# The state of a two-direction RWKV recurrence kept compact, its products over array quarters

## The chip, the cores and the metric

The kernel runs on one core of one Trainium2 chip, as one program. The metric is the device time of one execution in microseconds (us), the median of three runs. All arithmetic of the part in question is fp32.

## What is computed

The program is a transformer layer (a half feed-forward, a mixer of three attentions, another half feed-forward) followed by a second layer for the same 256 tokens of width 1024: a mixer of a long convolution ("hyena") and an RWKV-7 recurrence, then 16 experts that each choose 32 tokens. The change touches the recurrence alone. It runs twice: once over the 256 context tokens, for their final states only, and once over the 256 tokens of `x`, starting from those states and reading out every token. Each run goes in both directions, for 8 heads with a 64 x 64 state each.

```python
RW_HEADS = 8
RW_HEAD = 64
SCAN_DIRECTIONS = (False, True)

def rwkv_scan(decay, k, v, a_vec, b_vec, r, state0, reverse):
    emit = r is not None
    ...
    def step(S, inp):
        w_t, k_t, v_t, a_t, b_t = inp[:5]
        sa = jnp.einsum('bhij,bhj->bhi', S, a_t)
        S = S * w_t[:, :, None, :] + sa[..., None] * b_t[:, :, None, :] + v_t[..., None] * k_t[:, :, None, :]
        y = jnp.einsum('bhij,bhj->bhi', S, inp[5]) if emit else None
        return S, y
    S, ys = lax.scan(step, state0, xs, reverse=reverse)

def layer(x, ctx, c, c_ctx, p, ctx_out):
    ...
    ctx_states = rwkv_context_states(cols, p, zero_state)
    h = rmsnorm(x, p['norm1_pre']) * (1.0 + m_lat[1]) + m_lat[0]
    mixed, _ = token_mixer_2(h, p, ctx_states)
    x = x + m_lat[2] * rmsnorm(mixed, p['norm1_post'])
    h2 = rmsnorm(x, p['norm2_pre']) * (1.0 + m_lat[4]) + m_lat[3]
    x = x + m_lat[5] * rmsnorm(expert_choice_moe(h2, p), p['norm2_post'])
```

## The kernel before

The recurrence is worked in chunks of 64 tokens (`CH`), four steps (`NCH`) per run. In each step both directions advance by one chunk, the forward one from the front, the backward one from the back, so that the two chunks of a step always lie in opposite halves of the 128 partitions (`r`). Eight heads are kept as four pairs `p` with two heads `e` each; a feature lies on partition `e*64 + i`.

`rwkv` (L942) has three parts. First, for each direction and each half of the tokens, `elementwise` (L1009) forms decays and keys on ACT, DVE and POOL, and `products` (L1064) forms what doesn't depend on the state: masked 64 x 64 products (L1079), the transposed keys `TB` and `kt` (L1090, L1093), the products `MV` (L1098, evacuated at L1103), and the key-value products of both chunks, `pk` (L1109). These are 64 x 128 x 128 (contraction, rows of the output, columns): a pair of heads at a time, of which only the two diagonal 64 x 64 blocks are wanted; four ACT copies of 64x256 take them into `KV` (L1115). Second, a triangular solve: 31 rounds of a DVE product and sum (L1136, L1138), with trips through DRAM before and after (L1129, L1139, L1143), and block products (L1167, L1175) whose evacuations (L1182, L1184) finish the tiles `W`.

Third, the four steps (L1201 on). The state of a direction is a block-diagonal tile of 128 x 4 x 2 x 64, half of it zeros, in a ring of two (`ring`, zeroed at L1193, loaded from `Sctx` at L1191). A step multiplies the state by the decay and adds `KV` on POOL, in halves (`se`, L1213 and L1215, eight instructions of 64x256), multiplies the state by the inputs (`pu`, L1218, eight products of 128 x 64 x 128), adds `MV` on DVE (`u`, L1221), multiplies by `W` (`pz`, L1227, sixteen products of 64 x 64 x 64), copies on ACT (`z`, L1230, a copy for each direction), forms the update (`pn`, L1236, eight products of 64 x 128 x 128, half of each unused), and adds `se` to its diagonal blocks on DVE (L1240, four of 64x256). The run over `x` also adds the state's and `z`'s shares to the output banks `psY` (L1245, L1250). `psT` and `psX` are pools of two PSUM banks each.

The order of work on each engine is made by a list scheduler from the program order and a timing model, with no order written out here; each engine then takes its list in order. The context run (`context_states`, L1261) is issued after the fifth block of the first feed-forward and lies beside that feed-forward's products (L299 to L302 for weight blocks of 256 columns, each weight split on ACT and DVE, L245 and L246) and the first projections of the attention (L287 to L289). The run over `x` (called in `mixer2`, L1471) lies beside the projections and the transform of the long convolution (L1382 to L1434), whose splits are shared by DVE and POOL (L271, L272), and later beside the gate projections. After `psY` comes a normalisation (L1531 on), the output projection, the router, and the experts, whose 384 weight blocks of 1 MB come on SP's queue (L1774) through a ring of SBUF slots.

## Time and profile before

| what | value |
|---|---|
| median of three runs | 2164.89 us (2160.2 to 2174.39) |
| the profiled execution's own time | 2165.86 us |
| its span, first to last instruction | 2164.1 us |
| outside the span | 1.8 us |
| TensorE's mean granted clock, of full speed | 0.868 |
| busy: PE, PEld, DVE, ACT, POOL | 80%, 48%, 41%, 27%, 16% of the span |

PE is TensorE's matmul, PEld its weight load, DVE VectorE, ACT ScalarE, POOL GpSimd, SP SyncE. An fp32 product of the code is two MATMUL records. A row of windows gives the stretch (us from the span's start), its length, then the busy us (and instructions) of PE, PEld, DVE, ACT and POOL, TensorE's granted clock as a share of full speed, the DMA engines' busy share and GB/s. Windows of a line alone give the engines that it uses, then clock and DMA of the whole stretch. A row of a timeline gives start, duration, engine, line, operation, output and inputs, shapes (a product's as contraction*rows, then the moving operand), a count, and in brackets the idle time before it. A row of the chain gives start, duration, engine, tile, line.

### The profile page before, as it was taken

Reading aid. Unit: us, or ns where it says so; the run is one execution under the profiler, and the core shown is the slowest. Engines: PE = TensorE matmul, PEld = TensorE weight load, DVE = VectorE, ACT = ScalarE, POOL = GpSimd, SP = SyncE. Lnnn points to the kernel's source line nnn. Section 1 sums busy time; section 2 is a strip of 40 time slices with the busy share of each in tenths; the row PEclk is TensorE's granted clock in tenths of the full one; section 3 lists DMA queues with packets and bytes.
Section 4 is the critical chain, followed back from the end, with each engine's and each line's share of the span. In section 5 each row is a group of like instructions: output and inputs, shape, how many; then the busy total and the mean of one; then the engine's idle time right before and its main releaser. Section 6 shows DMA issues by size and latency. Waiting matters only on the chain.

```text
span 2164.1 us, 28403 instructions
## 1 busy us (share of the span) xinstructions
PE 1736.5 (80%) x11441; PEld 1048.8 (48%) x11442; DVE 885.5 (41%) x1611; ACT 579.1 (27%) x938; POOL 335.5 (16%) x332
## 2 busy tenths in 40 slices
PE   7999989999988999898898876666666665766675
PEld 5889867777768887887577511111111110111110
DVE  4668765875758665687756400000000000000001
ACT  3346443544436544454323200000000000000000
POOL 2111013210325640235233200000000000000000
PEclk9999998999999999999898887877777768677766
DMA  9665555454448855534445899999999999999996
GB/s 303 217 184 142 159 147 177 138 146 127 136 146 269 274 194 174 156 94 124 121 137 218 338 420 420 420 420 420 420 420 420 419 420 419 420 420 420 420 419 270
DMA packets 187894, 600.95 MB, mean 278 GB/s; under 512 B 35384, under 2 KB 91217, under 8 KB 138610
## 3 DMA queue, kind: packets, MB, share of 16 engines
q1 hardware_dynamic: 151312, 551.89, 67.5%
q0 software_dynamic: 10496, 36.08, 5.0%
q10 hardware_dynamic: 25954, 11.16, 1.9%
q8 instruction: 90, 1.47, 0.3%
q14 instruction: 42, 0.34, 0.0%
HBM read 593.25 MB, written 9.75 MB: 279 GB/s over the span
## 4 chain that ended last, share of the span: by engine, by line
DMA 45%; PE 37%; DVE 9%; ACT 3%; issue 3%; POOL 2%; ACTq 0%; DVEq 0%; SPq 0%; POOLq 0%
DMA ring<-exp_w 42%; PE mm L302 4%; PE mm L301 4%; PE mm L299 4%; PE mm L287 3%; PE mm L288 3%; PE mm L289 3%; DVE wl L246 3%; PE mm L346 2%; PE mm L349 2%; PE mm L345 2%; DMA wraw<-w_in 1%; ACT wh L245 1%; PE mm L254 1%; PE px L839 1%
## 5 line engine op out<-in xcount | busy, mean ns | idle before, releaser
L1789 PE MATMUL px<-ring,xeT 128*32 128x512 f32 x2048 | 356.7, 789 | 185.2 <-DMA ring<-exp_w 185.2
L246 DVE TENSOR_TENSOR wl<-wraw,wh 128x1024 fp32r<-128x1024 f32 (+2 forms) x243 | 317.2, 1307 | 167.4 <-ACT wh L245 163.3
L245 ACT ACTIVATE wh<-wraw 128x1024 fp32r<-128x1024 f32 (+2 forms) x243 | 254.5, 1048 | 372.4 <-PE mm L301 156.0
L302 PE MATMUL mm<-hh,wl 128*128 128x256 f32 x912 | 267.0, 294 | 16.5 <-DVE wl L246 15.5
L1789 PEld LDWEIGHTS px<-ring,xeT 128*32 128x32 f32 x2048 | 49.9, 122 | 465.5 <-DMA ring<-exp_w 390.1
L299 PE MATMUL mm<-hh,wh 128*128 128x256 f32 x912 | 265.4, 292 | 2.7 <-ACT hh L245 2.4
L301 PE MATMUL mm<-hl,wh 128*128 128x256 f32 x912 | 263.5, 289 | 1.9 <-DVE hl L246 1.7
L1825 PE MATMUL tr<-ring,hid 128*32 128x512 f32 x1024 | 182.1, 813 | 101.8 <-DMA ring<-exp_w 89.1
L1801 DVE SCALAR_TENSOR_TENSOR mth<-mth,px 128x512 f32<-128x512 f32 x16 | 11.0, 687 | 556.7 <-ACT mth L1800 556.7
L302 PEld LDWEIGHTS mm<-hh,wl 128*128 128x128 f32 x912 | 178.4, 196 | 31.6 <-DVE wl L246 20.4
L299 PEld LDWEIGHTS mm<-hh,wh 128*128 128x128 f32 x912 | 179.0, 196 | 12.1 <-issue 6.9
L301 PEld LDWEIGHTS mm<-hl,wh 128*128 128x128 f32 x912 | 179.2, 197 | 7.0 <-issue 4.1
L1829 ACT ACTIVATE ye<-tr 128x512 f32<-128x512 f32 x16 | 9.6, 597 | 559.6 <-PE tr L1825 559.6
L1635 POOL TENSOR_SCALAR rsz<-ss 128x1 f32<-128x1 f32 x2 | 0.6, 300 | 930.8 <-ACT ring L1635 930.7
L1825 PEld LDWEIGHTS tr<-ring,hid 128*32 128x32 f32 x1024 | 26.1, 127 | 238.1 <-DMA ring<-exp_w 209.5
L288 PE MATMUL mm<-wl,hh 128*128 128x512 f32 (+2 forms) x320 | 128.2, 401 | 3.5 <-DVE wl L246 2.0
L289 PE MATMUL mm<-wh,hl 128*128 128x512 f32 (+2 forms) x320 | 126.0, 394 | 0.0
L287 PE MATMUL mm<-wh,hh 128*128 128x512 f32 (+2 forms) x320 | 119.3, 405 | 5.2 <-DVE wi L525 3.3
L1802 DVE SCALAR_TENSOR_TENSOR mth<-mth,px 128x512 f32<-128x512 f32 x16 | 11.0, 688 | 252.6 <-PE px L1789 252.6
L1800 ACT ACTIVATE mth<-px 128x512 f32<-128x512 f32 x16 | 9.5, 597 | 281.2 <-PE px L1789 281.2
L288 PEld LDWEIGHTS mm<-wl,hh 128*128 128x128 f32 x320 | 61.4, 192 | 18.9 <-DVE wl L246 3.2
L287 PEld LDWEIGHTS mm<-wh,hh 128*128 128x128 f32 x320 | 59.4, 193 | 20.5 <-issue 7.7
(757 smaller groups left out, 2661.9 us busy)
## 6 DMA issues: line engine op xcount, KB each, us to landing
ring<-exp_w SPq DMA_DIRECT2D x384, 1024.0 KB
wraw<-w_in SPq DMA_DIRECT2D x107, 512.0 KB
mraw<-mod_w POOLq DMA_DIRECT2D x48, 512.0 KB, 5.2
wraw<-ffn_w_gate SPq DMA_DIRECT2D x44, 512.0 KB
wraw<-ffn_w_up SPq DMA_DIRECT2D x44, 512.0 KB
wraw<-ffn_w_down SPq DMA_DIRECT2D x44, 512.0 KB
wraw<-w_out SPq DMA_DIRECT2D x11, 512.0 KB
skew<-bd POOLq DMA_DIRECT2D x1, 3840.0 KB, 26.0
```

The costliest lines, as they stand in the source:

```text
L245: S.activation(dst_h, src, AF.Copy)
L246: (eng or V).tensor_tensor(dst_l, src, dst_h.bitcast(F32), op=ALU.subtract)
L287: PE.matmul(ps[t], hh[:, k, sl], wh, start=(k == 0), stop=False)
L288: PE.matmul(ps[t], hh[:, k, sl], wl, start=False, stop=False)
L289: PE.matmul(ps[t], hl[:, k, sl], wh, start=False, stop=(k == kc - 1))
L299: PE.matmul(o(c), wh[:, cs], hh[:, k, :], start=(k == 0 and bank0(c)), stop=False, skip_group_check=True)
L301: PE.matmul(o(c), wh[:, cs], hl[:, k, :], start=False, stop=False, skip_group_check=True)
L302: PE.matmul(o(c), wl[:, cs], hh[:, k, :], start=False, stop=(k == KC - 1), skip_group_check=True)
L345: PE.matmul(acc[t][nh], fh[:, sl], wh[:, ns], start=(k == 0), stop=False)
L346: PE.matmul(acc[t][nh], fh[:, sl], wl[:, ns], start=False, stop=False)
L1789: PE.matmul(ps[32 * g:32 * g + 32, :], xeT[:, k, es], wt[:, 0, g * 512:(g + 1) * 512], start=(k == 0), stop=(k == KC - 1), skip_group_chec ...
L1825: PE.matmul(pe2[32 * c:32 * c + 32, :], hid[:, 2 * h + j, 32 * g:32 * g + 32], w2t[:, j * 2 + nh, :], start=(g == 0 and h == 0), stop=(g = ...
```

## The change

The state of both directions becomes one compact tile `S_` of 128 x 2 x 4 x 64 without zeros. `pu` becomes sixteen products of 64 x 64 x 64 into two banks, by head of the pair `e` (the row half of the array), with one DVE sum for each bank. The key-value products leave `products`: the transposed keys of both directions stay in `KT`, and each step starts two banks `pn` with sixteen key-value products of 64 x 64 x 64; the update products, sixteen of 64 x 64 x 64, add to the same banks. In both, `p`, `d`, `e` are run through so that four products in a row use the four quarters of the array, each row half with a bank of its own. `se` becomes one POOL product of 128x512, `z` one ACT copy, the new state two DVE sums of 128x256. `MV` is sorted by steps, so that its evacuation is two ACT copies of 64x512 instead of one of 128x512. The last step of the run over `x` forms no new state. The run over `x` keeps block-diagonal copies `Sb` of the state for the `psY` products, made by four ACT copies of 64x256 in each of three steps; at the start, four memsets and five DMAs instead of two and two. The compact tiles take the SBUF of `e` and `kt` (the latter is also the solve's `pr`), the copies that of the old ring.

```diff
-        MV = [(stage or rp).tile([128, 2, 512], F32, name=f"MV{d}") for d in range(2)]
-        KV = [(stage or rp).tile([128, NCH, 4, 64], F32, name=f"KV{d}") for d in range(2)]
+        MV = [(stage or rp).tile([128, 2, 512], F32, name=f"MV{i}") for i in range(NCH // 2)]
+        KT = [(stage or rp).tile([128, 2, 512], F32, name=f"KV{d}") for d in range(2)]
...
-            kt = rp.tile([128, 512], F32, name="kt")
-            V.tensor_copy(kt, f2(ps))
+            V.tensor_copy(KT[d][:, t, :], f2(ps))
...
-            S.activation(MV[d][:, t, :], ps, AF.Copy)
-            pk = [psT.tile([128, 4, 128], F32, name="tr"), psX.tile([128, 4, 128], F32, name="px")]
-            for p in range(4):
-                hs = slice(p * 128, p * 128 + 128)
-                for cc in range(2):
-                    r = slice(cc * 64, cc * 64 + 64)
-                    PE.matmul(pk[cc][:, p, :], kt[r, hs], vt[r, t, hs], start=True, stop=True, skip_group_check=True)
             for cc in range(2):
-                ps = pk[cc]
+                r = slice(cc * CH, cc * CH + CH)
                 step = t * 2 + cc if d == 0 else NCH - 1 - (t * 2 + cc)
-                for e_ in range(2):
-                    f = slice(e_ * 64, e_ * 64 + 64)
-                    S.activation(KV[d][f, step], ps[f, :, e_ * 64:e_ * 64 + 64], AF.Copy)
+                S.activation(MV[step // 2][r, step % 2, :], ps[r], AF.Copy)
...
-        ring = [[rp.tile([128, 4, 2, 64], F32, name="S_", tag=tg) for tg in tgs]
-                for tgs in (("thw0", "tha0"), ("lam0", "km0"))]
-        for i, r_ in enumerate(ring):
-            for d, q_ in enumerate(r_):
-                if i == 1 and S0 is not None:
-                    S.dma_start(q_.rearrange("p a b c -> p (a b c)"), S0[d])
-                else:
-                    G.memset(q_, 0.0)
+        ring = [rp.tile([128, 2, 4, 64], F32, name="S_", tag=tg) for tg in ("e", "kt")]
+        blk = []
+        if emit:
+            blk = [[rp.tile([128, 4, 2, 64], F32, name="Sb", tag=tg) for tg in tgs]
+                   for tgs in (("thw0", "tha0"), ("lam0", "km0"))]
+            for q_ in blk[0] + blk[1]:
+                G.memset(q_, 0.0)
+            S.dma_start(ring[1].rearrange("p a b c -> p (a b c)"), Sctx)
+            for d in range(2):
+                for e in range(2):
+                    f = slice(e * 64, e * 64 + 64)
+                    S.dma_start(blk[1][d][f, :, e, :], Sctx[f, d * 256:d * 256 + 256].rearrange("f (p v) -> f p v", p=4))
...
-        S_ = ring[1] if S0 is not None else None
-
-        def ev(st):
-            return st.rearrange("p e v -> p (e v)")
+        S_ = ring[1] if emit else None
+        def pev(ap):
+            return ap.rearrange("q (p e v) -> q p e v", e=2, v=64)
...
-            u, z = uu[:, step % 2], zz[:, step % 2]
+            u, z, mv = uu[:, step % 2], zz[:, step % 2], MV[step // 2][:, step % 2]
+            ends = emit and step == NCH - 1
+            if not ends:
+                pn = [psX.tile([128, 4, 64], F32, name="px") for _ in range(2)]
+                def to_state(left, right, first):
+                    for p in range(4):
+                        for d, t, r in where:
+                            for e in range(2):
+                                hs = slice((2 * p + e) * 64, (2 * p + e) * 64 + 64)
+                                PE.matmul(pn[d][e * 64:e * 64 + 64, p, :], left(d, t)[r, hs], right(t)[r, hs],
+                                          start=(first and p == 0), stop=not first, skip_group_check=True)
+                to_state(lambda d, t: KT[d][:, t], lambda t: vt[:, t], True)
             if S_ is not None:
-                se = rp.tile([128, 2, 4, 64], F32, name="se", tag="nn")
-                pu = psT.tile([128, 512], F32, name="tr")
-                for d, t, r in where:
+                if not ends:
+                    se = rp.tile([128, 2, 4, 64], F32, name="se", tag="nn")
+                    G.tensor_tensor(se, S_, EC[:, :, :, step:step + 1].to_broadcast([128, 2, 4, 64]), op=ALU.mult)
+                pu = [psT.tile([128, 4, 64], F32, name="tr") for _ in range(2)]
+                for p in range(4):
                     for e in range(2):
                         f = slice(e * 64, e * 64 + 64)
-                        G.tensor_tensor(se[f, d], S_[d][f, :, e, :],
-                                        EC[f, d, :, step:step + 1].to_broadcast([64, 4, 64]), op=ALU.mult)
-                        G.tensor_tensor(se[f, d], se[f, d], KV[d][f, step], op=ALU.add)
-                for p in range(4):
-                    for d, t, r in where:
-                        PE.matmul(pu[r, p * 128:p * 128 + 128], AR[t, d][:, p, 0, r], ev(S_[d][:, p]), start=True,
-                                  stop=True, skip_group_check=True)
-                for d, t, r in where:
-                    V.tensor_tensor(u[r], pu[r], MV[d][r, t, :], op=ALU.add)
+                        for d, t, r in where:
+                            PE.matmul(pu[e][r, p, :], AR[t, d][f, p, 0, r], S_[f, d, p, :], start=True, stop=True,
+                                      skip_group_check=True)
+                for e in range(2):
+                    V.tensor_tensor(pev(u)[:, :, e], pu[e], pev(mv)[:, :, e], op=ALU.add)
+            else:
+                u = mv
             pz = psT.tile([128, 512], F32, name="tr")
             for h in range(8):
                 hs = slice(h * 64, h * 64 + 64)
                 for d, t, r in where:
-                    ur = u[r] if S_ is not None else MV[d][r, t, :]
-                    PE.matmul(pz[r, hs], W[t, d][r, h % 2, h // 2, 0, :], ur[:, hs], start=True, stop=True,
+                    PE.matmul(pz[r, hs], W[t, d][r, h % 2, h // 2, 0, :], u[r, hs], start=True, stop=True,
                               skip_group_check=True)
-            for d, t, r in where:
-                S.activation(z[r], pz[r], AF.Copy)
-            Sn = ring[step % 2]
-            pn = [psX.tile([128, 4, 128], F32, name="px") for _ in range(2)]
-            for p in range(4):
-                hs = slice(p * 128, p * 128 + 128)
-                for d, t, r in where:
-                    PE.matmul(pn[d][:, p, :], TB[d][r, t, hs], z[r, hs], start=True, stop=True, skip_group_check=True)
-            for d, t, r in where:
-                for e in range(2):
-                    f = slice(e * 64, e * 64 + 64)
-                    V.tensor_tensor(Sn[d][f, :, e, :], pn[d][f, :, e * 64:e * 64 + 64],
-                                    se[f, d] if S_ is not None else KV[d][f, step], op=ALU.add)
+            S.activation(z, pz, AF.Copy)
+            if not ends:
+                to_state(lambda d, t: TB[d][:, t], lambda t: z, False)
+                Sn = ring[step % 2]
+                for d in range(2):
+                    if S_ is not None:
+                        V.tensor_tensor(Sn[:, d], pn[d], se[:, d], op=ALU.add)
+                    else:
+                        V.tensor_copy(Sn[:, d], pn[d])
             if emit:
+                Sb = blk[(step + 1) % 2]
                 for p in range(4):
                     for d, t, r in where:
-                        PE.matmul(psY[t][r, p * 128:p * 128 + 128], AR[t, d][:, p, 1, r], ev(S_[d][:, p]),
-                                  start=False, stop=False, skip_group_check=True)
+                        PE.matmul(psY[t][r, p * 128:p * 128 + 128], AR[t, d][:, p, 1, r],
+                                  Sb[d][:, p].rearrange("q e v -> q (e v)"), start=False, stop=False,
+                                  skip_group_check=True)
                 for h in range(8):
                     hs = slice(h * 64, h * 64 + 64)
                     for d, t, r in where:
                         PE.matmul(psY[t][r, hs], W[t, d][r, h % 2, h // 2, 1, :], z[r, hs], start=False,
                                   stop=False, skip_group_check=True)
+                if not ends:
+                    for d in range(2):
+                        for e in range(2):
+                            f = slice(e * 64, e * 64 + 64)
+                            S.activation(blk[step % 2][d][f, :, e, :], Sn[f, d], AF.Copy)
             S_ = Sn
...
-    Sctx = dram.tile([2, 128, 512], F32, name="Sctx")
+    Sctx = dram.tile([128, 512], F32, name="Sctx")
...
-            S_, _, _, _ = rwkv(rp, c, None, zk, zv, zl, None, None)
-            for d in range(2):
-                S.dma_start(Sctx[d], S_[d].rearrange("p a b c -> p (a b c)"))
+            S_, _, _, _ = rwkv(rp, c, None, zk, zv, zl, None)
+            S.dma_start(Sctx, S_.rearrange("p a b c -> p (a b c)"))
```

## Rows read from the trace of the kernel before

**Rows 1.** The page's chain that ended last, by engine

```profile
DMA 45%; PE 37%; DVE 9%; ACT 3%; issue 3%; POOL 2%; ACTq 0%; DVEq 0%; SPq 0%; POOLq 0%
```

**Rows 2.** Windows by stage, all engines: see the columns above

```profile
150.00:217.00 67.00, 66.40 (x785) 61.97 (x785) 52.73 (x73) 43.21 (x93) 11.37 (x15) 1.00 0.47 133
...
307.00:365.00 58.00, 49.75 (x370) 39.32 (x369) 33.61 (x59) 20.31 (x33) 24.00 (x31) 0.88 0.33 93
950.00:1020.00 70.00, 65.15 (x837) 58.81 (x836) 53.04 (x78) 33.22 (x70) 35.85 (x33) 0.96 0.44 120
...
1056.00:1083.00 27.00, 20.34 (x333) 13.89 (x331) 15.91 (x33) 5.17 (x14) 6.74 (x7) 0.81 0.34 89
1083.00:1141.00 58.00, 56.94 (x507) 45.79 (x508) 31.30 (x47) 16.81 (x22) 21.48 (x28) 1.00 0.41 137
...
1244.00:2146.00 902.00, 590.05 (x3181) 102.12 (x3178) 39.25 (x80) 25.57 (x49) 0.00 (x0) 0.75 1.01 418
```

**Rows 3.** Windows of L1109 alone, the key-value products

```profile
150.00:217.00 67.00, 3.97 (x48) 3.20 (x48) 1.00 0.47 133
...
950.00:1020.00 70.00, 5.40 (x64) 4.25 (x64) 0.96 0.44 120
```

**Rows 4.** Windows of L1218 alone, the state products `pu`

```profile
307.00:365.00 58.00, 4.13 (x48) 2.95 (x48) 0.88 0.33 93
...
1083.00:1141.00 58.00, 4.72 (x48) 3.25 (x48) 1.00 0.41 137
```

**Rows 5.** Windows of L1236 alone, the update products `pn`

```profile
307.00:365.00 58.00, 8.79 (x64) 7.63 (x64) 0.88 0.33 93
...
1083.00:1141.00 58.00, 9.24 (x64) 7.71 (x64) 1.00 0.41 137
```

**Rows 6.** Timeline of PE: batches of small products

```profile
163.61 0.97 PE L1079 MATMUL px<-ar,tha 64*64 64x64 f32 x32
...
1077.27 1.29 PE L1175 MATMUL px<-nb,Bs 32*32 32x32 f32 x128
...
1084.83 1.16 PE L1236 MATMUL px<-zk,tb 64*128 64x128 f32 x8
...
1096.86 1.15 PE L1227 MATMUL tr<-uu,nb 64*64 64x64 f32 x32
```

**Rows 7.** Chain of waits, full-size products behind a small batch

```profile
1098.01 0.43 PE mm L287
1098.44 0.23 PE mm L288
```

**Rows 8.** Timeline of POOL, 305 to 330 us

```profile
316.20 0.61 POOL L1213 TENSOR_TENSOR se<-S__2191,ec 64x256 f32<-64x256 f32 x1
...
318.94 0.56 POOL L217 TENSOR_TENSOR rsi<-rsz,power 128x1 f32<-128x1 f32 x1
```

**Rows 9.** Timeline of POOL, 974 to 1008 us

```profile
988.43 1.75 POOL L1213 TENSOR_TENSOR se<-S__10208,ec 64x256 f32<-64x256 f32 x2
990.26 2.23 POOL L1215 TENSOR_TENSOR se<-se,KV 64x256 f32<-64x256 f32 x2
992.57 1.89 POOL L1048 TENSOR_TENSOR x<-x,zk 128x512 f32<-128x512 f32 x1
```

**Rows 10.** Timeline of POOL, 1052 to 1090 us: one 128x512 operation

```profile
1064.43 1.26 POOL L1421 TENSOR_TENSOR yf<-yf,hyt 128x512 f32<-128x512 f32 x1
```

**Rows 11.** Groups by line and shape, 900 to 1180 us: evacuations of `pk`

```profile
L1115 ACT ACTIVATE KV<-px 64x256 f32<-64x256 f32 x8 | 3.0, 379 | 0.1
```

**Rows 12.** Timelines of DVE, then ACT, around the solve's end

```profile
1055.40 0.19 DVE L1138 TENSOR_TENSOR tx<-tx,pr 128x31 f32<-128x31 f32 x1
...
1080.21 1.30 ACT L1182 ACTIVATE nb<-px 32x256 f32<-32x256 f32 x4 [8.82 <-DVE nb L1184]
```

**Rows 13.** Timeline of DVE, the last step's state sums

```profile
1135.13 0.87 DVE L1240 TENSOR_TENSOR S__10208<-px,se 64x256 f32<-64x256 f32 x2
```

**Rows 14.** Timeline of SP: the expert weights' stream

```profile
1150.91 147.92 SPq L1774 DMA_DIRECT2D ring<-exp_w  x54
```

More of the change, by code (lines that the diff above doesn't have):

```diff
@@ L940, in mix_take, with rwkv @@
         return take
-    def rwkv(rp, c, zr, zk, zv, zl, S0, alt, stage=None):
+    def rwkv(rp, c, zr, zk, zv, zl, alt, stage=None):
         emit = zr is not None
@@ L1470, in mixer2 @@
                 rp = f2.enter_context(tc.tile_pool(name="rw", bufs=1))
-                _, psY, vt, prod = rwkv(rp, c, zr, zk, zv, zl, [Sctx[0], Sctx[1]],
+                _, psY, vt, prod = rwkv(rp, c, zr, zk, zv, zl,
                                         [x_[:, h * 512:h * 512 + 512].rearrange("p (a b) -> p a b", a=4)
```

## The prediction, made before the changed kernel was run

> **What bounds the kernel now.** I read the chain that ended last first: waits for DMA hold 45% of the span, TensorE 37%, all else little [rows 1]. Then the windows by stage, to see where each of the two rules. From 1244 us to 2146 us the DMA engines are busy without a gap at 418 GB/s [rows 2]: the experts' weights set the end there, and nothing in the recurrence can shorten that stretch. But the stream's first issue is at 1150.91 us [rows 14], behind the whole mixer, so a stage ahead of it that ends sooner moves the stream, and the end with it, by as much. In the stages ahead TensorE rules, not evenly: it is busy 66.40 of 67 us where the context run forms its products, 49.75 of 58 where its steps run, 65.15 of 70 where the products for `x` are formed, 20.34 of 27 in the solve's tail, and 56.94 of 58 where the steps for `x` run beside the gate projections [rows 2]. Where it is full, a microsecond of products less is a microsecond less; where it waits, what ends the waits has to be looked at.
>
> **The products that go.** The change replaces three kinds. Key-value products, L1109: the 48 records from 150 to 217 us take 3.97 us, 83 ns each, so the context run's 64 take about 5.3 us; for `x` 64 take 5.40 us [rows 3]. State products, L1218: 4.13 us for the context's three steps, 4.72 us for three of the four steps for `x` [rows 4]. Update products, L1236: 8.79 and 9.24 us [rows 5]; the four of one direction, 8 records, take 1.16 us [rows 6]. In all 5.3 + 5.4 + 4.1 + 4.7 + 8.8 + 9.2 = 37.5 us, with the fourth `pu` for `x` (about 1.6 us at the rate of the other three) 39.1 us.
>
> **The products that come.** A batch of sixteen products of 64 x 64 x 64 is 32 records. Context: four key-value batches, three `pu`, four updates, 11 batches. For `x`: three, four and three, 10 batches. No row shows such a batch spread over four quarters; the nearest bound it. `pz` has the very shape, on two quarters: 32 records in 1.15 us, 36 ns each; two quarters under one row half take 0.97 us [rows 6]. Were the quarters to work one at a time, a record would take twice the 36 ns and a batch 2.3 us. Were all four to work at once, half of 1.15: 0.58 us; the 32 x 32 x 32 products, which run through four places of the array, take 1.29 us for 128 records, 10 ns each [rows 6], so the array does take records faster than one in 36 ns. I take 0.58 us for updates: `z` now comes in one ACT copy, so both directions are ready together and the written order `p`, `d`, `e` can stand. For key-value and `pu` I take 1.15 us: the new state comes by two DVE sums, one direction after the other, `pn`'s banks come free the same way, and a list that takes what is ready first runs one direction, two quarters, before the other. That makes 7 x 0.58 + 14 x 1.15 = 20.2 us, so TensorE is relieved of 18.9 us; with all batches at 0.58 us it would be 27, with all at 1.15 us 15, and one at a time 39.1 - 48.3 = 9 us more than before.
>
> Now by stages, since not all of that is time.
>
> **Context products (150 to 217 us and just behind).** 5.3 us of L1109 go, with four ACT copies of 379 ns in each of four calls [rows 11]; the second `MV` copy gives some of that back. TensorE is full here, and I count 85% of its part: **4.5 us**. Bounds: 0 if the feed-forward's weight splits then set the pace (DVE is busy 52.73 of 67 us [rows 2]), 6 if the ACT copies had also held up the banks.
>
> **Context steps (307 to 365 us).** 4.13 + 8.79 = 12.9 us become 7 x 1.15 + 4 x 0.58 = 10.4; at TensorE's 86% share the 2.5 us are worth 2.1. A second gain is on POOL. The row `rsi` at 318.94 us belongs to the norm ahead of the attention, and from 316.20 us it stands behind four half-size decay operations, 2.7 us [rows 8]. The change leaves one operation a step; a 128x512 on POOL took 1.26 us [rows 10], and `rsi` may still have to let it pass. I count 1.5 of the 2.7. Together **3.6 us**; bounds 0 to 9 (four quarters throughout, all of POOL's wait gone).
>
> **Products for `x` (950 to 1020 us).** The POOL operations of step 0 stand at 988.43 and 990.26 us, between `elementwise`'s own work, and the key product L1048 starts only when they are through, at 992.57 us: 4.1 us [rows 9]. The new `se` needs the state from DRAM, whose tile is now the solve's `pr`; that comes free at 1055.4 us [rows 12], so the operation leaves this place altogether. Against it stand two more memsets, about half a microsecond each, estimated from the 1.26 us of a two-input 128x512 operation. The 5.40 us of L1109 lie on an engine busy 93% of the stage, but partly in the shadow of the same POOL wait: I count half, 2.7. Together 4.1 - 1.0 + 2.7 = **5.8 us**; bounds 1 (DVE, 53.04 of 70 us busy, takes over) and 9.
>
> **Solve's tail (1056 to 1083 us).** The state's load, `se` and the first `pu` now come after 1055.4 us. `pz` can't start before the last evacuation L1182 of 1080.21 us [rows 12], 25 us later; a DMA, a product batch of 1.15 us and two sums fit in, and TensorE is idle 6.7 us of this stage. **Nothing**; if that cover went, up to 3 us. On ACT the loads stand beside those of the solve: two DMA issues became five.
>
> **Steps for `x` (1083 to 1141 us).** 4.72 + 9.24 = 14.0 us go; three key-value and three `pu` batches at 1.15 and three updates at 0.58 come, 8.6 us. TensorE is 98% full: **5.3 us**. The last step forms no state, so its two pairs of sums, the first 0.87 us [rows 13], also leave DVE's list ahead of the normalisation; I count them as hidden. The twelve ACT copies for `Sb`, 12 x 0.379 = 4.5 us by [rows 11], lie on an engine busy 16.81 of 58 us and are wanted one step later: nothing, and 4.5 us at most without that cover. Bounds 1.5 to 9.
>
> **A cost of changing shapes.** The first full-size product behind a small batch takes 0.43 us, the next 0.23 [rows 7]: 0.2 us for each return. The key-value batches left `products`, where other small ones stood beside them, and are now seven places more in the steps: 7 x 0.2 = **1.4 us** at worst, which I take. The Trainium skill, "TensorEngine Tiling (Array Packing)", section Tiling Modes, says that a change of the tiling mode drains TensorE. The row agrees: by that rule, too, the new batches cost extra wherever a full-size product lies between, and the sum is the same 1.4 us.
>
> **Sum.** 4.5 + 3.6 + 5.8 + 0 + 5.3 - 1.4 = 17.8 us, against the profiled execution's own 2165.9 us: 2148 us. That execution is 1 us above the median of the runs shown, within their spread, so I correct nothing: **2148 us**. The experts' stage is left as it is, only earlier.
>
> **Rivals.**
> *All four quarters at once.* TensorE is relieved of 27 us, not 19. For it: the 10 ns per record of the 32 x 32 x 32 batches; a bank for each row half. Against: readiness by direction. The context's steps then take 11 x 0.58 = 6.4 us in place of 10.4, worth 6.5 x 0.86 = 5.6, and with all of POOL's 2.7 us 8.3; the steps for `x` 9 x 0.58 = 5.2 in place of 8.6, worth 8.8; and of L1109's 5.4 us for `x` 5.0 count at TensorE's 93%, with 4.1 - 1.0 of POOL 8.1. That gives 4.5 + 8.3 + 8.1 + 8.8 - 1.4 = 28.3 us less: 2138 us. The Trainium skill's same page, section Tiling Modes (Key Properties), says that different tiles can load and multiply in parallel; by that rule this rival would hold, and the trace bears it out for two quarters only.
>
> *The relief goes into waiting.* Weight splits on DVE and ACT, or the list's new order, keep the pace of the feed-forward and of the convolution's projections: the context stages and 950 to 1020 us give nothing, and only the steps for `x` keep 5.3 - 1.4 us: 2162 us. For it: DVE at 79% and 76% beside TensorE [rows 2]. Against: TensorE at 99% in the first.
>
> *Key-value products in the steps' way.* `pn`'s two banks are held from a step's start to its sums, and the next step's key-value batch waits for the sums just as `pu` does, so it stands ahead of `pu` in every step. If the quarters work one at a time, each batch is 2.3 us, and all 21 stand in the chain of the steps: 48.3 us, in place of 4.1 + 6.3 + 8.8 + 9.2 = 28.4 us of old `pu` and updates there. What left the product stages, 70% of L1109's 10.7 us and POOL's 4 us, gives back 11.5: 48.3 - 28.4 - 11.5 = 8.4 us more, 2174 us. It decides from a batch of 39.9 / 21 = 1.9 us on. Against: two quarters of `pz` do overlap.
>
> **Chances.** Forecast 0.40, four quarters 0.30, waiting 0.22, in the way 0.08. About 1% (21.6 us) is what a measurement of this kernel can tell from no change: below 2143 lies nearly all of the second case and a quarter of the first, 0.38; above 2186 only the far end of the last case, with the list's order worse than now as well, 0.05; the rest, 0.57, is within 1%. The range runs from four quarters with the upper bounds of the four stages (6 + 9 + 9 + 9 = 33 us, and 3 us of shorter waits) to no gain at all and 2 us more: 2130 to 2168. The forecast's own is 2141 to 2157.
>
> **What would show it.** After: key-value and `pu` batches near 1.15 us, updates near 0.6; TensorE's busy time 19 us lower, its share in the step stages no lower; L1048 no longer behind `se`; the stream's first issue some 18 us earlier and its stretch as long as before. Batches over 1.9 us, a longer gap ahead of the norm's `rsi` or of `pz`, or a stream that starts where it did would prove it wrong.

## The result, and the profile after

The changed kernel takes 2135.77 us, median of four runs (2127.84 to 2137.52), beside 2166.75 us before: a ratio of 0.9845 (95% interval 0.9821 to 0.9869), some 33 us less by the ratio and 31 by the medians. Timed again on another occasion it gave 2133.44 us and 0.9856 (0.9833 to 0.9880). The forecast of 17.8 us less had the sign, its range holds the time, and it was some 13 us short.

The page of the changed kernel: the busy time of each engine, then the chain that ended last.

```profile
PE 1710.0 (80%) x11745; PEld 1024.6 (48%) x11746; DVE 867.6 (41%) x1593; ACT 571.9 (27%) x918; POOL 291.4 (14%) x280
...
DMA 44%; PE 38%; DVE 10%; ACT 3%; issue 3%; POOL 1%; ACTq 1%; SPq 0%; DVEq 0%; POOLq 0%
```

TensorE is busy 26 us less (1736.5 us before), POOL 44 us less (335.5). The chain is what it was [rows 1]: nothing new bounds the kernel, everything ahead of the stream is earlier.

Windows of the changed kernel, all engines, over the stages of [rows 2], moved by as much as each has become earlier.

```profile
150.00:217.00 67.00, 65.73 (x803) 61.00 (x804) 53.67 (x75) 39.78 (x83) 9.55 (x11) 1.00 0.47 138
307.00:365.00 58.00, 49.31 (x582) 40.19 (x581) 30.47 (x69) 19.96 (x35) 10.50 (x12) 0.91 0.48 141
...
1073.00:1122.00 49.00, 44.37 (x675) 35.38 (x674) 22.23 (x36) 17.21 (x27) 7.11 (x7) 0.93 0.46 154
1218.00:2120.00 902.00, 595.71 (x3198) 101.33 (x3186) 39.17 (x80) 25.58 (x49) 0.00 (x0) 0.75 1.01 419
```

In the steps for `x` TensorE was full before, 98%; now it is 91% busy. It has become faster than what feeds it, and something there makes it wait. The experts' stretch is as long as before.

The batches are the second thing to read. Timelines of PE at the first step for `x` that updates a state: the kernel before, then the changed one.

```profile
1084.83 1.16 PE L1236 MATMUL px<-zk,tb 64*128 64x128 f32 x8
1085.92 0.67 PE L1250 MATMUL mm<-zk,nb 64*64 64x64 f32 x8
1086.52 1.16 PE L1236 MATMUL px<-zk,tb 64*128 64x128 f32 x8
1087.61 1.14 PE L1250 MATMUL mm<-zk,nb 64*64 64x64 f32 x24
```

```profile
1078.89 0.69 PE L1213 MATMUL px<-zk,tb 64*64 64x64 f32 x32
1079.41 1.11 PE L1256 MATMUL mm<-zk,nb 64*64 64x64 f32 x32
...
1081.35 0.71 PE L1213 MATMUL px<-vt,KV 64*64 64x64 f32 x32
1081.86 0.66 PE L1225 MATMUL tr<-S__10177,ar 64*64 64x64 f32 x32
```

Two update batches of 1.16 us, one for each direction, have become one of 0.69 us. The products of `W` and `z` behind them (L1250, now L1256), which the change doesn't touch and the forecast doesn't name, have also drawn together: 0.67 and 1.14 us became 1.11. Key-value and `pu` batches take 0.71 and 0.66 us and start 0.51 us apart.

By stages, from the starts of one instruction that ends each, in profiles of the kernel before, of the changed one, and of the changed one's second occasion (us):

| stage, up to | before | changed | again | difference | forecast |
|---|---|---|---|---|---|
| first attention product (L592) | 379.6 | 371.7 | 367.4 | -7.9, -12.2 | -8.1 |
| second mixer's `zk` (L936) | 516.6 | 520.7 | 520.6 | +4.1, +4.0 | 0 |
| solve's last copies (L1182, now L1173) | 185.0 | 178.2 | 181.3 | -6.8, -3.7 | -5.8 |
| first gated output (L1541, now L1551) | 69.2 | 58.3 | 58.5 | -10.9, -10.7 | -5.3 |
| first expert product (L1789, now L1799) | 73.7 | 70.7 | 70.7 | -3.0, -3.0 | 0 |
| end of span | 940.0 | 936.1 | 938.6 | -3.9, -1.4 | 0 |

The forecast's 1.4 us for changes of shape are in none of its rows. The second row is code that the change leaves alone; with the old context run it took 513 to 520 us in four of the experiments below, with the new one 517 to 522 in seven, so its 4 us are near what it scatters, or a part of the context's gain given back. The last row's are near its scatter, too (937 to 940 in the twelve experiments). What is left to explain above all is the steps for `x`: twice their term.

That row ends at the gated output, and the last products of the gate projections cross this mark. Timelines of PE, the last of them in the kernel before, then in the changed one:

```profile
1150.25 0.39 PE L289 MATMUL mm<-wh,hl 128*128 128x512 f32 x1
```

```profile
1134.09 0.39 PE L289 MATMUL mm<-wh,hl 128*128 128x512 f32 x1
```

Before, this product starts 0.1 us ahead of the gated output, in the changed kernel 5.2 us behind it. From the solve's last copies to it, it is 69.0 us before, 63.5 in the changed kernel and 63.8 again: 5.5 us less for nearly the same work of TensorE. The other 5.4 us of the row come from the order of the work.

### The profile page after: what moved, and what is told of

It reads as the page before. It is cut to its first block, busy times and chain, and to the rows that moved or that the text cites. A ratio compares the mean times of both kernels' runs of the same rounds, so it can differ in the third digit from the quotient of the medians.

```text
span 2135.7 us, 28907 instructions
## 1 busy us (share of the span) xinstructions
PE 1710.0 (80%) x11745; PEld 1024.6 (48%) x11746; DVE 867.6 (41%) x1593; ACT 571.9 (27%) x918; POOL 291.4 (14%) x280
## 4 chain that ended last, share of the span: by engine, by line
DMA 44%; PE 38%; DVE 10%; ACT 3%; issue 3%; POOL 1%; ACTq 1%; SPq 0%; DVEq 0%; POOLq 0%
DMA ring<-exp_w 41%; PE mm L302 4%; PE mm L299 4%; PE mm L301 4%; PE mm L287 3%; PE mm L288 3%; PE mm L289 3%; DVE wl L246 3%; PE mm L346 2%; PE mm L349 2%; PE mm L345 2%; ACT wh L245 1%; PE px L1799 1%; PE mm L254 1%; PE px L839 1%
## 5 line engine op out<-in xcount | busy, mean ns | idle before, releaser
L1799 PE MATMUL px<-ring,xeT 128*32 128x512 f32 x2048 | 361.7, 797 | 185.6 <-DMA ring<-exp_w 185.5
L302 PE MATMUL mm<-hh,wl 128*128 128x256 f32 x912 | 266.8, 294 | 17.5 <-DVE wl L246 14.5
L1799 PEld LDWEIGHTS px<-ring,xeT 128*32 128x32 f32 x2048 | 49.5, 122 | 470.3 <-DMA ring<-exp_w 400.3
L1835 PE MATMUL tr<-ring,hid 128*32 128x512 f32 x1024 | 185.5, 828 | 96.4 <-DMA ring<-exp_w 83.8
L299 PEld LDWEIGHTS mm<-hh,wh 128*128 128x128 f32 x912 | 179.4, 197 | 14.4 <-issue 7.1
```

The costliest lines, as they stand in the source:

```text
L299: PE.matmul(o(c), wh[:, cs], hh[:, k, :], start=(k == 0 and bank0(c)), stop=False, skip_group_check=True)
L302: PE.matmul(o(c), wl[:, cs], hh[:, k, :], start=False, stop=(k == KC - 1), skip_group_check=True)
L1799: PE.matmul(ps[32 * g:32 * g + 32, :], xeT[:, k, es], wt[:, 0, g * 512:(g + 1) * 512], start=(k == 0), stop=(k == KC - 1), skip_group_chec ...
L1835: PE.matmul(pe2[32 * c:32 * c + 32, :], hid[:, 2 * h + j, 32 * g:32 * g + 32], w2t[:, j * 2 + nh, :], start=(g == 0 and h == 0), stop=(g = ...
```

## The experiments

The theory at the outset was the forecast's: what TensorE is spared counts where it is full, and POOL's shorter list counts ahead of L1048 and `rsi`. Its rivals: four quarters at once make the gain; or the shorter lists and waits of ACT, DVE and POOL do.

**The whole change again**, as the measure for the three kernels timed beside it (one quarter, two copies of `z`, copies for `Sb` twice).

> The whole change once more, as the measure for the runs beside it: by its first comparison 0.985 of before, some 33 us faster. If that holds it comes within 5 us of 2136 us.

Measured: 2133.44 us, 0.9856, within what was expected; its stages stand in the table above.

**Each run of the recurrence alone.** The new code for the context run and the old for `x`, and the reverse.

```diff
...
-            S_, _, _, _ = rwkv(rp, c, None, zk, zv, zl, None, None)
+            S_, _, _, _ = rwkv_new(rp, c, None, zk, zv, zl, None)
...
```

> Only the context run has the new recurrence; the run over x is the old one (the context's final state is copied into the old block form first). The trace of the whole change has the attention start 7.9 us earlier and the second mixer's projections 3.8 us earlier. If gains of the context run pass through to the end undiminished: 8 us below the kernel before, about 2159 us. If the feed-forward and the attention give half of it back as the trace of the whole change has it: 4 us below, 2163 us. If the context's part is hidden altogether: 2166 us.

> Only the run over x has the new recurrence. By the landmarks of the whole change 24 to 25 of the 28 us arise behind the second mixer's projections: about 2142 us. By the prediction's own terms for that part (5.8 and 5.3 us, or 8.1 and 8.8 us with four quarters at once) 2150 to 2155 us. Together with e1 the two gains should add up to the whole one (31 us by the medians) if they are independent.

Measured: 0.9933 (0.9914 to 0.9952) with the context run new, 14.5 us less; 0.9905 (0.9881 to 0.9929) with the run over `x` new, 20.6 us less. Together that is 35 us, the whole change within the intervals. The context run is worth nearly twice the highest guess, 8 us. The run over `x` lies between its two guesses, and is worth twice what the forecast's terms had for it (5.8 + 5.3 - 1.4 = 9.7 us).

**Two quarters, then one quarter at a time.** The loops of the 21 batches turned, nothing else.

```diff
-                    for p in range(4):
-                        for d, t, r in where:
+                    for d, t, r in where:
+                        for p in range(4):
```

> The whole change, with the loops of the small products turned round: key-value and update products run one direction after the other (one row half, two quarters at a time), the state products one head of the pair after the other. Batches then take about 1.1 us instead of 0.69, TensorE about 9 us more in all. If four quarters at once is where the gain comes from: 7 to 10 us slower than the whole change, 2143 to 2146 us. If the gain comes from the shorter lists of the other engines and shorter waits: 0 to 3 us slower.

> The whole change with the loops of its 21 batches turned so that four products in a row use one quarter of the array. If quarters then work one at a time, a batch of 32 records takes 1.5 to 2.3 us in place of 0.69. If TensorE's load in the steps sets the time, the kernel is 12 to 25 us slower than the whole change, above all between the solve's end and the gated output. If that load is hidden, as two quarters at a time (0.97 us a batch, no slower) suggested, it stays within 4 us.

Measured: two quarters 2136.52 us, 0.9847 (0.9826 to 0.9868), the whole change's own ratio, although batches took 0.97 us where they stand undivided; one quarter 2141.71 us, 0.9895 (0.9875 to 0.9916), 8 us more than the whole change beside it, between the two cases expected, with batches of 1.5 us. The two intervals of that pair just touch. TensorE's time in the three kinds of batches (windows over both runs' steps) is 15.5 us in the whole change, 21.6 and 30.2 here: 6 us more of TensorE cost nothing that can be told, 15 us more cost 8. And the steps for `x`, from the solve's last copies to the first gated output, don't follow the load: 58.3 and 58.5 us in the whole change, 60.3 with two quarters (3.6 us more of these batches in there), 55.8 with one (6.7 us more). A part of this is the mark: with two quarters 5.9 us of the stage are products of the long convolution's transform (L1437), which the whole change and the kernel with one quarter have ahead of it. The kernel with only the run over `x` new, whose code is the whole change's here, takes 59.9 us, 6.5 of them such products (L1757). An estimate without them, as TensorE is busy for 59.1 of the 60.3 and 57.8 of the 59.9 us: 53.4 us with only `x` new, 54.4 with two quarters, 55.8 with one quarter, but 58.3 in the whole change. So slower batches cost 1 to 2.4 us in this stage, and the whole change has some 5 us that the other three don't have. The waits show where. TensorE's waits between the solve's end and the first gated output: the kernel before, the changed one, two quarters, one quarter (us in total, times, longest).

```profile
PE mm L287 <- ACT yfh L245: 1.0, 1, 1.0
PE tr L1227 <- ACT nb L1182: 0.4, 1, 0.4
...
```

```profile
PE mm L287 <- DVE gg L1521: 3.9, 1, 3.9
PE px L1213 <- ACT zk L1237: 0.7, 1, 0.7
...
```

```profile
PE mm L287 <- DVE gg L1521: 1.0, 1, 1.0
...
```

```profile
PE mm L289 <- DVE yfl L246: 0.3, 1, 0.3
```

A wait for `gg` that isn't there before takes up a part of what TensorE gains. It is short with two quarters, 1.3 us with only the run over `x` new, and gone with one quarter. The changed kernel's timeline of POOL tells where it comes from, and its timeline of PE and windows what it costs besides.

```profile
1095.42 2.04 POOL L1518 TENSOR_TENSOR vt<-vt,bs 128x512 f32<-128x512 f32 x2
1097.41 0.58 POOL L206 DMA_DIRECT2D lnb<-rw_ln_b  x1
1104.09 2.48 POOL L1519 TENSOR_TENSOR vt<-vt,lnb 128x512 f32<-128x512 f32 x2 [6.10 <-DMA lnb<-rw_ln_b]
```

```profile
1106.71 0.79 PE L287 MATMUL mm<-wh,hh 128*128 128x512 f32 x1 [3.94 <-DVE gg L1521]
1107.31 0.63 PE L288 MATMUL mm<-wl,hh 128*128 128x512 f32 x1
1107.73 0.63 PE L289 MATMUL mm<-wh,hl 128*128 128x512 f32 x1
```

```profile
1107.00:1112.00 5.00, 5.00 (x12) 3.51 (x11) 1.55 (x4) 0.00 (x0) 0.00 (x0) 0.50 0.29 105
```

The new `ring` lives in the tags `e` and `kt`. `kt` was free after the solve before, and `lnb` uses it: its load was issued at 1057.44 us. Now it stands behind the last reader of the state of step 2, is issued at 1097.41, and lands 6 us after POOL wants it. POOL adds this row, the normalisation's bias, to `vt`; DVE then multiplies `vt` by the output gate's product in the bank `pg` and forms `gg` from it, and only then does the bank come free. So `vt`, `gg` and the bank come late, and the next gate product with them. Behind that idle stretch TensorE's granted clock is 0.50, the level of 1.2 GHz, for the next twelve products, which start 0.43 us apart in place of 0.23: 2.4 us more. In the kernel with two quarters the wait is 1.0 us and the window from 1107 to 1112 us has clock 1.00. So in the whole change wait and clock cost these steps 3.9 + 2.4 = 6.3 us, about 5 us more than the same wait at full clock in the kernels with two quarters or only `x` new. The profile repeated on the second occasion has the same wait, 4.0 us, and the same twelve slow products. This is read from traces; a version with `lnb` elsewhere wasn't tried. Where the kernel with one quarter loses its 8 us wasn't located: its profile is 2.8 us longer than the whole change's second one, and not in this stage.

**One copy of `z`.** Alone in the kernel before, and undone in the changed one.

```diff
-            for d, t, r in where:
-                S.activation(z[r], pz[r], AF.Copy)
+            S.activation(z, pz, AF.Copy)
```

> The kernel before, with one ACT copy of z for both directions in place of one for each. Both directions' updates are then ready together, so records of the two row halves can alternate, as L1109's did at 83 ns a record, where before L1236's took 137 to 144 ns. If readiness by direction made the update dear, L1236's sum falls by some 7 us and the kernel is 4 to 7 us faster. If the 128-wide shape does, L1236 keeps its 137 ns or more and the time stays within 2 us.

> The whole change with z copied from its bank by two ACT operations, one for each direction, as before. If the single copy is what makes a batch of updates run at once, updates split into two batches of 16 records, each two quarters wide, and with the compact shape they cost 0.3 to 0.5 us more a step: 2 to 4 us in all, half of what it cost the kernel before (9 us there). If the compact shape alone sets it, no change within 2 us.

Measured: alone 2156.89 us, 0.9956 (0.9941 to 0.9971), 9.5 us less than before; undone 2155.26 us (2146.26 to 2160.28), 0.9949 (0.9927 to 0.9971), 20 us more than the whole change beside it. The timeline of PE of the kernel before with one copy:

```profile
1098.57 1.16 PE L1235 MATMUL px<-zk,tb 64*128 64x128 f32 x16
1099.66 1.15 PE L1249 MATMUL mm<-zk,nb 64*64 64x64 f32 x32
```

Sixteen update records of both directions now take the 1.16 us of one direction's eight, without a change of shape. L1236's sum falls from 18.0 to 10.3 us, L1250's from 7.1 to 4.6: 10 us of TensorE for one copy. In the changed kernel with two copies L1257 is back at 6.5 us (4.5 in the whole change) and updates at 3.3 for `x` (2.1), and the wait for `gg` is 6.7 us:

```profile
PE mm L287 <- DVE gg L1522: 6.7, 1, 6.7
```

The profiled execution, at 2146, is the fastest of this kernel; what the others lose beyond it no trace shows. Expected were 2 to 4 us: the copy was taken for a help to the updates alone.

**Key-value products left ahead.** Compact state, but key-value products stay in `products`, are copied, and are added on POOL.

```diff
+                S.activation(KV[step // 2][:, step % 2, d], pk[cc], AF.Copy)
...
+                    G.tensor_tensor(se, se, KV[step // 2][:, step % 2], op=ALU.add)
```

> Compact state and 64x64x64 products, but the key-value products stay where they were, ahead of the steps, as 64x64x64 over four quarters, with one ACT copy of 128x256 for each chunk, and POOL adds them to the decayed state (two operations of 128x512 a step instead of one). If the rate of the small products is what counts: within 3 us of the whole change. If the sum in the banks, which spares copies, sums and two PSUM banks in the product stage, is what counts: 6 to 12 us slower than the whole change.

Measured: 2143.25 us, 0.9873 (0.9854 to 0.9893). By ratio that is 4 to 6 us more than the whole change's two comparisons, between the two cases expected; the intervals overlap, so a gain from adding up in the banks is possible and not shown.

**POOL's list.** Eight decay operations a step in the changed kernel; and the kernel before with the starting state loaded late, so that step 0's operations leave their place ahead of L1048.

```diff
...
-                for tgs in (("thw0", "tha0"), ("lam0", "km0"))]
+                for tgs in (("thw0", "tha0"), ("kt" if emit else "lam0", "km0"))]
```

> The whole change, with each step's decay on POOL done as four quarter-size operations, each of them twice: eight POOL operations a step as before, in place of one; the values are the same. If the shorter POOL list is part of the gain, the kernel is 4 to 8 us slower than the whole change and rsi of the norm behind the context run starts 1.5 to 3 us later. If the products on TensorE alone make the gain, it stays within 2 us of the whole change.

> The kernel before, with the forward direction's starting state for x in the buffer that the solve uses, so that it is loaded only behind the solve: the four POOL operations of step 0's forward half can then not stand ahead of the key product L1048. The products are the same. If POOL's place was part of the gain, as the forecast's 4.1 us had it, L1048 starts some 4 us earlier and the kernel is 3 to 4 us faster than before. If that wait was in the shadow of TensorE, it stays within 1.5 us, or is slower by what the late start of step 0 costs.

Measured: eight operations 2142.55 us, 0.9892 (0.9868 to 0.9917), 8 to 10 us above the whole change's 0.9856 and 0.9845, a little over the 4 to 8 expected, the intervals hardly overlapping. The late load: 0.9997 (0.9982 to 1.0012), nothing. Timelines at the context's norm, whose last sums come from `hid` on ACT: ACT, then POOL of the kernel with eight operations; ACT, then POOL of the changed kernel; then POOL of the kernel with the late load at its last L1048.

```profile
312.36 0.19 ACT L241 ACTIVATION_READ_ACCUMULATOR hid<-x 128x1 f32 x1
```

```profile
309.86 6.38 POOL L1223 TENSOR_TENSOR se<-S__2134,ec 64x256 f32<-64x256 f32 x8 [0.60 <-DVE S__2134 L1250]
316.33 0.30 POOL L214 TENSOR_SCALAR rsz<-ssq 128x1 f32<-128x1 f32 x1
316.72 0.57 POOL L217 TENSOR_TENSOR rsi<-rsz,power 128x1 f32<-128x1 f32 x1
```

```profile
316.06 0.18 ACT L241 ACTIVATION_READ_ACCUMULATOR hid<-x 128x1 f32 x1
```

```profile
316.35 0.50 POOL L214 TENSOR_SCALAR rsz<-ssq 128x1 f32<-128x1 f32 x1 [1.47 <-ACT hid L241]
316.93 0.56 POOL L217 TENSOR_TENSOR rsi<-rsz,power 128x1 f32<-128x1 f32 x1
```

```profile
994.29 1.80 POOL L1048 TENSOR_TENSOR x<-x,zk 128x512 f32<-128x512 f32 x1 [1.39 <-ACT x L1046]
```

`rsi` starts at 316.72 us behind eight operations and at 316.93 us in the changed kernel, but the norm's sums are done at 312.55 us in the one and at 316.24 in the other, so the two starts can't be compared by the clock of the page. Counted from the sums, `rsi` starts 4.2 us behind them with eight operations and 0.7 us in the changed kernel (0.7 again on the second occasion, 4.2 in the kernel before, whose sums end at 314.79 us). The first attention product follows: 58.8 us behind the sums with eight operations, 55.5 and 55.6 in the whole change's two profiles. So some 3 us of the price lie here, as the forecast had it. Another part is the wait for `gg`, 5.8 us in place of 3.9, as POOL reaches `vt` and `lnb` later; the rest wasn't located. And in the late-load kernel L1048 no longer waits for `se`, but for ACT 1.39 us: the next thing was late right behind it. Counted from the start of the second mixer's `zk`, it starts after 95.2 us, in place of 96.4; in the changed kernel it is 90.4. Of these 6 us the late load alone shows 1.2, and what makes the rest no run separates.

**The last state, and the copies for `Sb`.** The kernel before without the last step's state; the changed kernel with its twelve copies made twice.

```diff
...
-            for p in range(4):
+            for p in range(0 if ends else 4):
...
```

```diff
-                            S.activation(blk[step % 2][d][f, :, e, :], Sn[f, d], AF.Copy)
+                            for _ in range(2):
+                                S.activation(blk[step % 2][d][f, :, e, :], Sn[f, d], AF.Copy)
```

> The kernel before, without the new state of the last step for x, which nobody reads: its decay and key-value sums on POOL (1.5 us by the forecast's row of such operations and more by their count), its update products (2.3 us of TensorE) and its four sums on DVE (1.7 us ahead of the normalisation) are left out. If the end of the steps is set by the chain of DVE and POOL work behind the last products, the kernel is 3 to 5 us faster than before. If TensorE's load alone sets it, 2 us, which may not be told from nothing. If the last state was hidden, as the forecast counted its sums, no change within 1.5 us.

> The whole change with each of the twelve ACT copies into the block form of the state made twice, 12 times 0.415 us more on ACT. The forecast counted the copies as hidden: then no change within 2 us. If they lie on the path, the kernel is 3 to 5 us slower than the whole change, and the products of the next step that read the block form start later.

Measured: without the last state 1.0005 (0.9988 to 1.0022), nothing, as the forecast counted it. Copies twice: 2138.97 us, 0.9879 (0.9858 to 0.9900), 5.5 us above the whole change beside it, the intervals overlapping, so that a cost of the copies is likely and not shown. TensorE's waits in the steps of the kernel with the copies made twice:

```profile
PE mm L1250 <- ACT Sb L1263: 2.5, 4, 1.2
PE mm L287 <- DVE gg L1522: 2.0, 1, 2.0
...
```

The second set of copies stands in the way four times. The whole change's list of waits has no such row, so one set is hidden there, by little: with two quarters there is one such wait of 0.2 us.

## Why the prediction was right or wrong

**What bounds the kernel.** Right for the experts' stretch, which kept its 902 us. But the end does not move with the stream's first issue, as the forecast had it. Timelines of SP, all issues of the experts' weights: the kernel before, the changed one, the kernel with the late load.

```profile
1150.91 975.02 SPq L1774 DMA_DIRECT2D ring<-exp_w  x384
```

```profile
1134.10 966.80 SPq L1784 DMA_DIRECT2D ring<-exp_w  x384
```

```profile
1165.31 964.38 SPq L1774 DMA_DIRECT2D ring<-exp_w  x384
```

The first issue moved 16.8 us, near the 18 that the forecast named as its sign, while the span became 28.4 us shorter; with the late load the first issue is 14.4 us later than before, and the span 1.4 us longer. What the end goes with is the first expert product, which stands 936 to 940 us ahead of it in all fourteen profiles: that moved 24.5 us.

**Context products and steps, 8.1 us.** Right in kind and too small: 7.9 and 12.2 us in two profiles, 11.8 us in the profile of the context run alone, which is 14.5 us faster. "All four quarters at once" had 12.8 here. POOL's part, taken at 1.5 us, is borne out by the eight operations, at some 3 us.

**Products for `x`, 5.8 us.** Near in size (6.8 and 3.7, solve included), and its largest term isn't borne out: 4.1 us for POOL's place ahead of L1048 [rows 9]. Moving those operations alone gave nothing. The row was read to the end of one wait, and not to what ACT had ready by then.

**Solve's tail, nothing.** Not contradicted.

**Steps for `x`, 5.3 us, less 1.4.** The step that failed: 10.9 and 10.7 us to the gated output. The 5.5 us to the last gate product agree with the term by luck, as its parts don't. Windows over this stage give the account: before (all engines, then L1250 and L1245 alone), and after (all engines, then L1213, L1225, L1256 and L1250 alone).

```profile
1081.20:1150.40 69.20, 67.48 (x578) 54.44 (x578) 40.11 (x67) 22.19 (x29) 25.43 (x30) 1.00 0.41 137
1081.20:1150.40 69.20, 7.14 (x128) 1.00 0.41 137
1081.20:1150.40 69.20, 6.22 (x48) 1.00 0.41 137
```

```profile
1070.60:1128.90 58.30, 53.38 (x713) 42.72 (x714) 28.38 (x51) 21.54 (x34) 10.41 (x9) 0.94 0.45 150
1070.60:1128.90 58.30, 4.49 (x176) 0.94 0.45 150
1070.60:1128.90 58.30, 2.48 (x96) 0.94 0.45 150
1070.60:1128.90 58.30, 4.47 (x128) 0.94 0.45 150
1070.60:1128.90 58.30, 4.48 (x48) 0.94 0.45 150
```

The forecast's own lines went from 9.24 + 4.72 = 14.0 us [rows 4, 5] to 4.49 + 2.48 = 7.0, where it had 8.6: it put key-value and `pu` batches at 1.15 us, because the list would run one direction first, but they use all four quarters and take 0.71 and 0.66. Two lines that it left out shrank beside them, which before had run one direction at a time, too: `W` by `z` (L1250, now L1256) from 7.14 to 4.47 us, as one copy of `z` alone brought it to 4.6, and the products of the block state (L1245, now L1250) from 6.22 to 4.48, which is read from the traces only. That is 7.0 + 2.7 + 1.7 = 11.4 us of TensorE, twice the term. Then 25 records fewer of the projections' 144 stand in the stage, 5.8 us at 0.23 us each, most of them now behind the gated output; and the slow clock takes 2.4 us back. These add up to 14.8 us; by the windows TensorE's busy time fell by 14.1 us. Its idle time rose from 1.7 to 4.9 us, most of it the wait for `gg`, and 14.1 - 3.2 = 10.9. So TensorE was relieved of twice the term, a wait and a clock that the forecast didn't have took about half of it back, and the rest of the gain is the gated output's place ahead of the last gate products, where the forecast had counted TensorE's load alone. It moved the state into `kt` and asked when that tag comes free for it, not who has it next. The shape changes cost little: behind the batch at 1079.41 us the next full-size products start 0.34 and then 0.23 us apart, 0.11 us for a return, where 0.2 was taken. The kernel before has the same 0.34 us in its timeline, at 1097.94 us; the 0.2 came from the chain's row [rows 7].

**The rivals.** "All four quarters at once", 2138 us, is what came: the time, and the 0.6 to 0.7 us of its batches. That fits the rule of the Trainium skill, "TensorEngine Tiling (Array Packing)", section Tiling Modes (Key Properties), that tiles load and multiply in parallel, and here the trace shows it for four quarters. But the rate alone didn't make the time: with two quarters, at 0.7 of it, the kernel is as fast within what can be told. Something of "Into waiting" is true as well: 6.3 us went into a wait and the clock behind it, in a place that this rival didn't name. "In the way" would have needed batches of 1.9 us; at 1.5 us the kernel still beat the one before by 23 us.

**What made the gain.** Shown by runs: one copy of `z` (9.5 us alone, 20 with the rest). Likely, with intervals that touch: fewer POOL operations a step (8 to 10) and more than one quarter at a time (8). These are no shares of one sum, since each also moves the wait for `gg`. That the late load, which takes POOL's operations from their place ahead of L1048, and the last state give nothing alone, in the kernel before, is shown.

## What to carry to other kernels

When an evacuation is split in two, look at every product that reads it: products that could fill the array together run one half after the other, and the row that shows it is a batch of half the count with the whole duration. When a tile takes over a buffer's tag, ask who used that tag next; a load that was early becomes a wait late in the stage. When a slower variant is just as fast, list the waits of both before calling the work unimportant, and look which products have crossed the mark that ends a stage. And compare a start in two profiles by its distance from its own input, not by the time on the page.

## What was not expected of the hardware

Records of 64 x 64 x 64 over four quarters started 16 ns apart (32 in 0.51 us), 23 ns over two (26 in 0.59), 40 ns over one (29 in 1.15), with only the loops turned. And 3.94 us of idle on TensorE were followed by 5 us at a granted clock of 0.50, while 0.96 us at the same place, with two quarters, and 1.29 us, with only the run over `x` new, were followed by 1.00: the wait cost 1.6 times what its own row says.
